# Most of the latents' projection put behind the context's queries in the order of work, and three modulations of the second layer put into the first half of the gates

## The chip, the cores and the metric

The kernel runs on one core of one Trainium2 chip. It is written by hand for the core's engines: TensorE (PE, matrix products; its weight loads are listed as PEld), VectorE (DVE), ScalarE (ACT), GpSimd (POOL) and SyncE (SP), which issues most of the DMAs. Each engine takes its instructions strictly in the order in which they were laid down and waits at each until its operands are there. The metric is the device time of one execution in microseconds; lower is better. Three runs of the kernel before took 2460.11, 2469.60 and 4105.28 us; their median is 2469.6 us.

## The reference

Two layers of a backbone are applied to two groups of tokens that share all weights: 128 context tokens (one block of 128) and 256 latent tokens (two blocks). Everything is float32, and the model width is D = 1024. One layer computes, for either group:

```
mod = silu(cond) @ w_mod[l] + b_mod[l]           # six rows of D: shift1 scale1 gate1 shift2 scale2 gate2
h   = LN(x) * (1 + scale1) + shift1
p   = h @ w_in[l]                                # 1024 -> 1696 columns, for three mixers
A   = GQA attention, 8 query and 2 kv heads      # latents also attend to cached context keys
B   = multi-head latent attention, 4 heads
C   = chunked spatial-gating MLP
x   = LN(ALPHA*x + gate1 * (concat(A,B,C) @ w_o[l]))
h2  = LN(x) * (1 + scale2) + shift2
x   = LN(ALPHA*x + gate2 * PEER(h2))
```

PEER is a layer of 128 x 128 = 16384 single-neuron experts. For each token and each of 8 heads it forms a query `h2 @ w_q`, scores its two halves against 128 keys each, takes the best 16 of either, the best 16 of their 256 sums, and from these a softmax gate g. Then `out = sum over the 128 chosen experts of g * gelu(u[expert] . h2) * v[expert]`. The tables `u` and `v` are 16384 x 1024 for each layer. The outputs are the two groups' x after both layers and the context's new keys and values.

## The kernel before

**Two ways of computing PEER.** For the 128 context tokens only the chosen experts' rows are read: once the expert numbers `ids` are known (line 676), POOL issues 128 indirect DMAs for `u` (line 686), each of which brings one row of 4 KB for each of 128 tokens (512 KB) into one of four buffers `gt`, and DVE multiplies each with the context's `h2c` and sums it up (line 692, called a u_step below). Later 128 more such gathers bring rows of `v` (line 703). For the 256 latents the whole tables are streamed. The phase that goes through the first half of `u` is called phase A (`a_step`: SP loads, ACT and DVE split each block into a high and a low part, PE multiplies it with `h2T`, three passes, tile `psA`, line 854). Then 32 steps `w_step(0, n)` turn the gates of the first half of the experts into a dense matrix (tile `psW`, line 893) and multiply it in, in the first gate half; the product with `v` (`o_step`, tile `acc`, line 930) begins after them, and second halves of both follow.

**Order in a layer.** In a layer, the context's chain and the latents' chain run beside each other. The context's steps are marked as urgent (`hp()`): projection (`p`), attention (`a`), output projection and norm (`o`, line 522, tile `psoc`), then in `ctx_picks` the transposed and modulated h2 (line 201, tile `m2pst`), its queries (line 561, tile `psqp`, 16 chunks of `w_q`), the choice of experts (lines 546 to 643) and `ids`. The latents' projection `pl_` consists of 14 chunks of 128 columns of `w_in` (line 262, tile `psil`, one load `wil` a chunk; the last chunk has 32 columns). How many of them are written ahead of which of the context's steps is said by a string, `ORD` for the first layer and `ORD1` for the second: each `l` is one chunk, each digit one modulation of the first layer. What is left of the projection comes behind `ctx_picks` by `run(pl_)`. Then the latents' attention (lines 421 to 452, scores in `pssl`), output projection (line 522, tile `psol`; DVE takes each result at line 524) and second norm (line 147 on DVE and line 149 on ACT, tile `m2xh`) follow, then their queries with 16 more loads `wq`, routing, and phase A.

**Modulations.** A modulation is one of the six rows `mod`: 8 loads `wm` of 512 KB and 64 short matmuls (line 166, tile `psm`). Those of the second layer are taken from a list; `MB` of them are written ahead of the latents' attention of the first layer, the others later, one in each eighth step of a gate half.

**What sets the order.** A scheduler sorts the written steps by their urgency and a simulated time line into one fixed list for each engine. So an instruction stands behind all that were laid before it on its engine, also where they have nothing to do with each other: an attention step of the latents on DVE behind a u_step waits for that u_step's gather. All loads of weights go through SP's queue in one order, into a ring of six buffers of 512 KB (line 157); the context's `w_in` and `w_o` of the second layer have two buffers of their own. On POOL the first 50 gathers of the first layer and the first 60 of the second are free to go as soon as a buffer is free; each later one is tied to a mark in the latents' work (line 1028, `N0`). The store of the latents' x for the end of the layer (line 949, `xd`) stands in POOL's list among the gathers.

Of the kernel before, what the change touches and what calls it, by code (L numbers as in the profile page):

```python
# [45 lines left out]
def tile_fn(ctx: ExitStack, tc, A, outs):  # L46
# [17 lines left out]
    def psum(es, spec):  # L64

        for tag, n in spec.items():
            banks[tag] = pool(es, f"ps_{tag}", n, space=PSUM)

    def pS(tag, name):
        return banks[tag].tile([128, 512], F32, name=name, tag=tag)  # L70
# [575 lines left out]
    def out_c(cc):  # L646
        with ExitStack() as e1:
            cc.out_proj(e1)
# [100 lines left out]
    mods = []  # L749
    for l in range(DEPTH):  # L750
        last = l + 1 == DEPTH

        with ExitStack() as es3:
            psum(es3, BK[min(l, 1)])
            with ExitStack() as esc:
# [11 lines left out]
                def first():  # L767
                    run(project(l, cc))
                    if l == 0:
# [7 lines left out]
                       "a": lambda: cc.attention_in(esc), "o": lambda: out_c(cc)}  # L777
                for k in (ORD if l == 0 else ORD1):
                    if k == "l":
# [7 lines left out]
                if not last:  # L787
                    mods = [(l + 1, v) for v in (1, 0, 2, 4, 3, 5)]
                    for _ in range(MB):
                        modulation(*mods.pop(0), "m")  # L790
# [5 lines left out]
        with ExitStack() as es_:  # L796
# [158 lines left out]
            X = pool(es6, f"x{l}", 2)  # L955
            ar.append(pool(es6, f"at{l}").tile([128, NS - HALF, 256], F32, name="AR2"))
            psum(esP, {"acc": 4})
            accp = [[pS("acc", "acc") for _ in range(2)] for _ in range(2)]
            for n in range(NW):
                w_step(0, n)  # L960
                if (n + 1) * PRE // NW > n * PRE // NW:
                    a_step(NA + n * PRE // NW)
            for ii in range(PRE, NA):
                o_step(ii - PRE)
                a_step(NA + ii)
# [36 lines left out]
            for k, r in RATES[l].items():  # L1002
                ms = marks[k]
                n = int(len(ms) * r + 0.5)
# [22 lines left out]
CQ = 0  # L1027
RATES = [{'L':0.25,'A':1,'W':0.01,'B':2,'X':1,'O':2.125}, {'L':0.125,'A':0.875,'W':0.01,'B':2.375,'X':0.5,'O':2.625}]
N0 = [50,60]
MB = 5  # L1030
ORD1 = 'paollllllllllllll'
ORD = 'p2ll4ll3llaollllllll'
HP = 100000
KA = 0.125
KO = 0
# [92 lines left out]
```

## Time and profile before

| | before |
|---|---|
| median of three runs | 2469.6 us |
| profiled execution, own time | 2466.42 us |
| span of the profiled execution | 2464.7 us |
| granted clock of TensorE, mean | 0.961 of full speed |
| PE busy | 2267.0 us (92%) |
| DVE busy | 1959.7 us (80%) |
| ACT busy | 1166.0 us (47%) |
| POOL busy | 695.4 us (28%) |
| read from memory | 689.14 MB, 281 GB/s over the span |

All times in the rows below count from the first instruction of the profiled execution. What the execution's time adds to the span is 1.7 us. Busy time is the time in which an engine's own instructions ran; a share near one in a stretch says that the engine sets the pace there, a low share that it waits. In a timeline, the number in brackets is the engine's idle time just ahead of the row, with the instruction or DMA that ended it. Rows of equal instructions in sequence are drawn together, with their count at the end.

### The profile page before, as it was taken

To read this page: it belongs to the slowest core of one execution; us is meant where nothing else is said; L and a number is where in the kernel's file an instruction comes from. 1 tells how busy PE (TensorE), PEld (TensorE's weight loads), DVE (VectorE), ACT (ScalarE), POOL (GpSimd) and SP (SyncE) were. 2 spreads that over 40 slices of the span, in tenths; PEclk is the share of its full clock that TensorE was granted. 3 is DMA by queue.
4 is the path that set the end of the run, shared out by engine and by line. 5 is a ranking of instruction groups with operands and counts; after the bars stand their busy time and mean duration, and the time that the engine had idled before them with its cause. 6 is when DMAs were issued, how large, how long until landed. Compare 5 with 4: busy or idle time off the path is not lost. (4 is left out here: it accounts for less than half of the span.)

```text
span 2464.7 us, 42531 instructions
## 1 busy us (share of the span) xinstructions
PE 2267.0 (92%) x15980; PEld 1932.8 (78%) x15980; DVE 1959.7 (80%) x3995; ACT 1166.0 (47%) x2143; POOL 695.4 (28%) x523
## 2 busy tenths in 40 slices
PE   6999889899999999999989978689999999998997
PEld 5696568789997886677778856579999889965886
DVE  2157579997897889998853577899869888899987
ACT  3324422444785445544445342325448744465444
POOL 0000233443004554355100005432210053344640
PEclk8999989999999998999998989899999999998999
DMA  9857899889547999899763528888984499987994
GB/s 328 314 192 258 341 328 342 322 309 342 204 155 269 367 356 379 284 332 390 266 214 95 174 87 280 316 307 286 317 291 153 155 348 366 339 314 271 388 372 145
DMA packets 196318, 696.10 MB, mean 282 GB/s; under 512 B 22992, under 2 KB 27408, under 8 KB 196112
## 3 DMA queue, kind: packets, MB, share of 16 engines
q1 hardware_dynamic: 110016, 398.52, 45.3%
q0 software_dynamic: 74736, 272.14, 30.7%
q10 hardware_dynamic: 11360, 22.73, 2.7%
q8 instruction: 125, 2.05, 0.3%
q14 instruction: 81, 0.66, 0.1%
HBM read 689.14 MB, written 4.16 MB: 281 GB/s over the span
## 5 line engine op out<-in xcount | busy, mean ns | idle before, releaser
L686 POOL DMA_INDIRECT gt<-in_peer_u_dram,ids x256 | 303.0, 1183 | 1274.2 <-DVE ids L676 544.1
L854 PE MATMUL psA<-h2hi,ulo 128*128 128x256 f32 x1920 | 555.0, 289 | 32.3 <-DVE ulo L847 32.3
L854 PE MATMUL psA<-h2hi,uhi 128*128 128x256 f32 x1920 | 548.3, 286 | 5.6 <-ACT uhi L846 3.7
L854 PE MATMUL psA<-h2lo,uhi 128*128 128x256 f32 x1920 | 546.2, 284 | 0.0
L930 PE MATMUL acc<-vhi,pp 128*128 128x512 f32 x1856 | 521.1, 397 | 17.4 <-ACT pp L909 11.1
L686 POOL DMA_INDIRECT gt<-in_peer_v_dram,ids x256 | 388.1, 1516 | 432.3 <-DVE acc L703 383.1
L930 PEld LDWEIGHTS acc<-vhi,pp 128*128 128x128 f32 x1856 | 349.8, 191 | 93.8 <-ACT pp L909 11.6
L846 ACT ACTIVATE uhi<-u 128x1024 fp32r<-128x1024 f32 x240 | 254.5, 1060 | 345.9 <-PE psA L854 215.8
L854 PEld LDWEIGHTS psA<-h2hi,ulo 128*128 128x128 f32 x1920 | 370.7, 193 | 41.4 <-DVE ulo L847 40.9
L918 ACT ACTIVATE vhi<-v 128x1024 fp32r<-128x1024 f32 x232 | 246.1, 1061 | 319.6 <-PE acc L930 200.5
L854 PEld LDWEIGHTS psA<-h2hi,uhi 128*128 128x128 f32 x1920 | 370.8, 193 | 9.2 <-ACT uhi L846 4.7
L847 DVE TENSOR_TENSOR ulo<-u,uhi 128x1024 fp32r<-128x1024 f32 x240 | 292.7, 1219 | 106.4 <-ACT uhi L846 105.4
L854 PEld LDWEIGHTS psA<-h2lo,uhi 128*128 128x128 f32 x1920 | 370.6, 193 | 1.4
L703 DVE SCALAR_TENSOR_TENSOR acc<-gt,wcol,acc 128x1024 f32<-128x1024 f32 x254 | 324.5, 1278 | 7.5 <-DMA gt<-in_peer_v_dram,ids 6.7
L692 DVE SCALAR_TENSOR_TENSOR gt<-gt,h2c 128x1024 f32<-128x1024 f32 x256 | 309.7, 1214 | 23.3 <-DMA gt<-in_peer_u_dram,ids 21.9
L919 DVE TENSOR_TENSOR vlo<-v,vhi 128x1024 fp32r<-128x1024 f32 x232 | 282.7, 1220 | 57.2 <-ACT vhi L918 55.2
L930 PE MATMUL acc<-vlo,pp 128*128 128x512 f32 x928 | 295.9, 400 | 8.6 <-DVE vlo L919 7.5
L930 PEld LDWEIGHTS acc<-vlo,pp 128*128 128x128 f32 x928 | 174.3, 191 | 51.7 <-DVE vlo L919 15.0
L875 ACT ACTIVATE e<-iota,nid 128x128 f16<-128x128 f16 x512 | 158.8, 428 | 62.2 <-PE psW L893 62.0
L561 PE MATMUL psqp<-h2T,wq 128*128 128x256 f32 x512 | 119.6, 388 | 0.3 <-DVE h2T L207 0.3
L262 PE MATMUL psil<-wil,hT 128*128 128x128 f32 (+1 forms) x896 | 111.5, 276 | 0.8 <-ACT proj L263 0.5
L900 DVE SCALAR_TENSOR_TENSOR AR<-psW,AR 128x256 f32<-128x256 f32 (+2 forms) x256 | 96.0, 415 | 20.2 <-PE psW L893 20.0
(435 smaller groups left out, 2897.1 us busy)
## 6 DMA issues: line engine op xcount, KB each, us to landing
u<-in_peer_uT_dram SPq DMA_DIRECT2D x256, 512.0 KB
v<-in_peer_v_dram SPq DMA_DIRECT2D x256, 512.0 KB
wm<-in_w_mod_dram SPq DMA_DIRECT2D x96, 512.0 KB
wq<-in_peer_wq_dram SPq DMA_DIRECT2D x64, 512.0 KB
wic<-in_w_in_dram SPq DMA_DIRECT2D x26, 512.0 KB
wil<-in_w_in_dram SPq DMA_DIRECT2D x26, 512.0 KB
woc<-in_w_o_dram SPq DMA_DIRECT2D x16, 512.0 KB
wol<-in_w_o_dram SPq DMA_DIRECT2D x16, 512.0 KB
```

The costliest lines, as they stand in the source:

```text
L262: T.matmul(ps[:, :n], lhsT=ch.hT[b][:, c, :], rhs=wv[:, c, :], start=(c == 0), stop=(c == 7))
L561: T.matmul(ps[:, :n * 128], lhsT=wv[:, c, :], rhs=hT[:, c, :], start=(c == 0), stop=(c == 7))
L686: nc.gpsimd.indirect_dma_start(out=t, out_offset=None, in_=tab, in_offset=bass.IndirectOffsetOnAxis(ap=pk.ids[:, j:j + 1], axis=0))
L692: V.scalar_tensor_tensor(t, t, 1.0, pk.h2c, op0=OP.mult, op1=OP.mult, accum_out=acol[:, j:j + 1])
L703: V.scalar_tensor_tensor(pk.acc, t, wcol[:, j:j + 1], pk.acc, op0=OP.mult, op1=OP.add)
L846: S.activation(hi, ua, AF.Copy)
L847: marks["A" if ii < NA else "U" if ii < NA + PRE else "B"].append(V.tensor_sub(lo, ua, hi.bitcast(F32)))
L854: T.matmul(ps[:, a * 256:(a + 1) * 256], lhsT=lw[:, c * 128:(c + 1) * 128], rhs=rw[:, c, :], start=(k == 0), stop=(k == 8 * len(passes) - 1))
L875: S.activation(e2[:, t // TI, :, t % TI], iota1, AF.Abs, bias=nb_[:, t0 % 128 + t:t0 % 128 + t + 1])
L918: S.activation(hi, v, AF.Copy)
L919: marks["O" if ii >= NA else "Q" if ii >= NA - PRE else "P"].append(V.tensor_sub(lo, v, hi.bitcast(F32)))
L930: T.matmul(accp[tb][h], lhsT=pl[:, tb * 128:(tb + 1) * 128], rhs=vr[:, h * 512:(h + 1) * 512], start=(i == 0 and k == 0), stop=(i == 127 a ...
```

## The change

Four numbers and three lines of code change; lines after 960 move down by two.

```diff
@@ -955,11 +955,13 @@
             psum(esP, {"acc": 4})
-            accp = [[pS("acc", "acc") for _ in range(2)] for _ in range(2)]
             for n in range(NW):
                 w_step(0, n)
                 if (n + 1) * PRE // NW > n * PRE // NW:
                     a_step(NA + n * PRE // NW)
+                if n % 8 == 3 and len(mods) > 1:
+                    modulation(*mods.pop(0), "acc")
+            accp = [[pS("acc", "acc") for _ in range(2)] for _ in range(2)]
             for ii in range(PRE, NA):
@@ -1027,9 +1029,9 @@
-MB = 5
-ORD1 = 'paollllllllllllll'
-ORD = 'p2ll4ll3llaollllllll'
+MB = 2
+ORD1 = 'paollll'
+ORD = 'p2l4l3laolll'
```

In the first layer 6 of the 14 chunks of the latents' projection now stand ahead of the context's second norm and queries, not 14; in the second layer 4, not 14. The others come behind `ctx_picks` and ahead of the latents' attention. Of the second layer's modulations two, not five, stand ahead of the latents' attention in the first layer; three more come at n = 3, 11 and 19 of the first gate half, and the sixth in the second gate half as before. A modulation in the first gate half writes its sums to the four banks of `acc`, which is why `accp` is now taken behind that loop. No instruction is added or left out.

The scheduler turns this into new lists. Three places are shown, each row an instruction as `line operation output<-inputs shape`, with a count where equal ones follow one another.

On PE in the first layer, where the context's queries end, the list before ran the last pieces of the projection (`psil`) between the queries (`psqp`, scores `pssk`) and went on to the latents' scores (`pssl`):

```order
L561 MATMUL psqp<-h2Tc,wq_1755 128x128 x8
L262 MATMUL psil<-wil_1361,hT_536 128x32
L262 MATMUL psil<-wil_1361,hT_537 128x32 x3
L566 MATMUL pssk<-kT_1431,qp 128x128
L561 MATMUL psqp<-h2Tc,wq_1778 128x128 x8
L262 MATMUL psil<-wil_1361,hT_537 128x32 x4
L566 MATMUL pssk<-kT_1431,qp 128x128
L262 MATMUL psil<-wil_1361,hT_537 128x32
L421 MATMUL pssl<-kTl,qTl 128x384
```

Now, after the last query chunk (`wq_1602`), seven and a quarter chunks of projection and one modulation (`psm`) follow:

```order
L561 MATMUL psqp<-h2Tc,wq_1602 128x128 x8
L262 MATMUL psil<-wil_1734,hT_537 128x128 x4
L566 MATMUL pssk<-kT_1255,qp 128x128
L262 MATMUL psil<-wil_1734,hT_537 128x128 x4
L262 MATMUL psil<-wil_1756,hT_536 128x128 x8
L566 MATMUL pssk<-kT_1255,qp 128x128
L262 MATMUL psil<-wil_1756,hT_537 128x128 x8
L262 MATMUL psil<-wil_1778,hT_536 128x128 x4
```

The queries now run almost without projection between them, and `pssl` comes behind the last chunk (`wil_1888`) and the eight loads of modulation 1. In the second layer the same holds with nine and a quarter chunks and no modulation.

On DVE in the first layer, around the latents' first output projection (`psol`, line 524), the list before had these rows; the u_steps are those of line 692:

```order
L692 SCALAR_TENSOR_TENSOR gt,acol<-gt,h2c 128x1024
L423 TENSOR_REDUCE mx<-pssl 128x1
L171 TENSOR_TENSOR modrow<-psm,bm 128x256
L443 COPY pT<-psT 128x3x128
L427 RECIPROCAL sums<-sums 128x2
L692 SCALAR_TENSOR_TENSOR gt,acol<-gt,h2c 128x1024
L181 COPY cols_102<-psc 128x8 x2
L692 SCALAR_TENSOR_TENSOR gt,acol<-gt,h2c 128x1024
L524 TENSOR_TENSOR y_2840<-psol,g_2838 128x128
```

Now there are:

```order
L443 COPY pT<-psT 128x3x128
L692 SCALAR_TENSOR_TENSOR gt,acol<-gt,h2c 128x1024
L423 TENSOR_REDUCE mx<-pssl 128x1
L692 SCALAR_TENSOR_TENSOR gt,acol<-gt,h2c 128x1024
L427 RECIPROCAL sums<-sums 128x2
L692 SCALAR_TENSOR_TENSOR gt,acol<-gt,h2c 128x1024 x4
L524 TENSOR_TENSOR y_2664<-psol,g_2662 128x128
L524 TENSOR_TENSOR y_2665<-psol,g_2662 128x128
```

Counted from the start of the list, 8 u_steps stood ahead of the first row of line 524 and now 42; ahead of the latents' `m2xh` 19 and now 50; at the end of phase A 114 in either. In the second layer these are 15 and now 48, and 33 and now 60. POOL's list has 54 gathers ahead of the first `xd` store in the first layer, not 21, and 64 in the second, not 33.

On PE in the first gate half the second part of the first of the three modulations (`wm_2...`) now stands between two products of the gates (`psW`), and the other two later in the same way:

```order
L893 LDWEIGHTS e_5757
L893 MATMUL psW<-e_5759,e_5757 128x64
L166 MATMUL psm<-wm_22_5865,silu 32x256 x3
L166 MATMUL psm<-wm_23_5871,silu 32x256 x4
L166 MATMUL psm<-wm_24_5877,silu 32x256 x4
L166 MATMUL psm<-wm_25_5883,silu 32x256 x4
L166 MATMUL psm<-wm_26_5889,silu 32x256 x4
L166 MATMUL psm<-wm_27_5895,silu 32x256 x4
L893 LDWEIGHTS e_5907
L893 MATMUL psW<-e_5909,e_5907 128x64
```

Before, no row of line 166 stood there. On SP the loads go along: the first layer's queue had the 40 loads `wm` of five modulations between the context's `wq` and the `wol` of the latents' output projection, and has 16 now; the 24 others stand between the loads of `u` of the first gate half.

## Rows read from the trace of the kernel before

**Rows 1.** Page, parts 1 and 4: busy engines; chain of waits by engine.

```profile
PE 2267.0 (92%) x15980; PEld 1932.8 (78%) x15980; DVE 1959.7 (80%) x3995; ACT 1166.0 (47%) x2143; POOL 695.4 (28%) x523
...
PE 23%; DVE 8%; issue 4%; DMA 2%; POOL 2%; ACT 1%; DVEq 0%; POOLq 0%; ACTq 0%
```

**Rows 2.** Windows, layer 0 (columns: stretch, then each engine's busy us).

```profile
213.00:255.00 42.00, 39.72 (x312) 17.81 (x312) 34.48 (x161) 27.19 (x61) 0.00 (x0) 0.96 0.79 295
...
255.00:302.00 47.00, 41.55 (x278) 23.11 (x278) 24.58 (x61) 23.63 (x61) 13.02 (x12) 1.00 0.93 352
...
350.00:637.00 287.00, 266.77 (x1836) 252.86 (x1835) 256.38 (x716) 110.05 (x151) 112.54 (x92) 0.97 0.90 326
...
637.00:745.00 108.00, 105.56 (x1263) 104.66 (x1261) 98.81 (x177) 93.14 (x191) 0.00 (x0) 1.00 0.48 152
```

**Rows 3.** Timeline of PE, layer 0 (start us, us, instruction).

```profile
151.75 7.76 PE L262 MATMUL psil<-wil,hT 128*128 128x128 f32 x68
...
159.34 1.04 PE L201 MATMUL m2pst<-ident,m2xh 128*128 128x128 f32 x8
...
165.69 1.95 PE L561 MATMUL psqp<-h2Tc,wq 128*128 128x128 f32 x16
...
209.61 0.47 PE L566 MATMUL pssk<-kT,qp 128*128 128x128 f32 x2
...
210.15 0.91 PE L421 MATMUL pssl<-kTl,qTl 64*128 64x384 f32 x2
...
214.80 4.29 PE L166 MATMUL psm<-wm,silu 128*32 128x256 f32 x48
```

**Rows 4.** Timeline of SyncE's queue, layers 0 and 1: loads of weights.

```profile
200.28 76.51 SPq L157 DMA_DIRECT2D wm<-in_w_mod_dram  x40
...
1318.42 32.70 SPq L157 DMA_DIRECT2D wil<-in_w_in_dram  x8
```

**Rows 5.** Timeline of DVE, layer 0.

```profile
255.37 0.28 DVE L676 TENSOR_TENSOR ids<-i,i 128x128 int32<-128x128 f32 x1
...
303.79 0.29 DVE L524 TENSOR_TENSOR y<-psol,g 128x128 f32<-128x128 f32 x1 [5.01 <-PE psol L522]
...
336.14 0.81 DVE L147 TENSOR_SCALAR m2xh<-xl,m_mv,m_rs 128x1024 f32<-128x1024 f32 x1
```

**Rows 6.** Timeline of PE, layer 0: first matmul of the gates.

```profile
637.51 0.66 PE L893 MATMUL psW<-e,e 128*128 128x64 f16 x16
```

**Rows 7.** Timeline of PE and DVE, layer 1.

```profile
1387.66 1.07 PE L201 MATMUL m2pst<-ident,m2xh 128*128 128x128 f32 x8
...
1389.28 0.88 PE L421 MATMUL pssl<-kTl,qTl 64*128 64x384 f32 x2 [0.40 <-DVE gs L469]
...
1482.89 0.29 DVE L676 TENSOR_TENSOR ids<-i,i 128x128 int32<-128x128 f32 x1
...
1515.45 0.48 DVE L524 TENSOR_TENSOR y<-psol,g 128x128 f32<-128x128 f32 x2
...
1559.95 0.81 DVE L147 TENSOR_SCALAR m2xh<-xl,m_mv,m_rs 128x1024 f32<-128x1024 f32 x1
...
1846.42 0.66 PE L893 MATMUL psW<-e,e 128*128 128x64 f16 x16
```

**Rows 8.** Timeline of POOL, layer 1: gathers.

```profile
1483.45 0.93 POOL L686 DMA_INDIRECT gt<-in_peer_u_dram,ids  x1 [291.21 <-DVE ids L676]
...
1493.53 1.82 POOL L686 DMA_INDIRECT gt<-in_peer_u_dram,ids  x1 [1.14 <-DVE gt L692]
...
1547.93 1.02 POOL L686 DMA_INDIRECT gt<-in_peer_u_dram,ids  x1 [0.61 <-DVE la_rs L118]
```

**Rows 9.** Windows, layer 1.

```profile
1485.00:1545.00 60.00, 49.59 (x339) 40.82 (x338) 47.81 (x109) 13.47 (x33) 33.37 (x30) 0.94 0.88 302
...
1568.00:1848.00 280.00, 267.43 (x1868) 252.29 (x1867) 243.01 (x690) 109.74 (x151) 81.68 (x78) 0.98 0.86 303
```

**Rows 10.** Tile psm: what its engine waited for, us and times.

```profile
  DMA wm<-in_w_mod_dram: 46.9, 38
```

## The prediction

> **What bounds the kernel now.** I read the page first, then windows by stage, then the timelines of PE and DVE around the stages that the change touches, and last POOL's gathers. The page has PE busy 92% of the span, and the chain that ended last runs over PE for 23% and DVE for 8% [rows 1]. The windows show that this mean hides different stages [rows 2]. Between 213 and 255 us PE is busy 39.72 of 42 us: projection, queries and modulations set the pace. From 255 to 302 it is busy 41.55 of 47, DVE only 24.58, and the DMAs are at 0.93 with 352 GB/s. In phase A and the queries before it (350 to 637) PE is busy 266.77 of 287 and DVE 256.38, so either one delays the other. In the first gate half (637 to 745) PE is busy 105.56 of 108 and the DMAs only 0.48. So the change takes loads out of a stretch where they are dense and puts matmuls into one where PE has 2.4 us to spare.
>
> The points by which I measure are, in layer 0: the context's second norm reaches PE (`m2pst`) at 159.34, latents' scores begin at 210.15 [rows 3], `ids` at 255.37, first result of the latents' output projection at 303.79, latents' `m2xh` at 336.14 [rows 5], gates at 637.51 [rows 6]. In layer 1 the same points are 1387.66, 1389.28, 1482.89, 1515.45, 1559.95 and 1846.42 [rows 7].
>
> **Durations.** 68 matmuls of the projection start over 7.59 us (151.75 to 159.34) [rows 3], 0.112 us each; a chunk has 32, so 3.57 us. A query chunk of the context is 1.95 us and its score product up to 0.47 [rows 3]; I take 2.2. Modulation: 48 records `psm` in 4.29 us, 64 would be 5.7; where its loads are there, it is a little less, and I take 5 us. Gathers: 33 went out from 1483.45 to 1547.93 [rows 8], 64.48 / 32 = 2.015 us apart, with the DMAs at 0.88 and 302 GB/s in that stretch [rows 9]. That is the pace of gathers when nothing but gathers and the latents' attention runs, and I use it for the new lists, which ask for such a run in both layers.
>
> **Layer 0, up to the latents' second norm.** Three chunks fewer are loaded and multiplied ahead of the context's output projection and its norm; 3 x 3.57 is 10.7 us of PE, of which part filled gaps in the context's chain. I put `m2pst` 8 us earlier, at 151. From there to the first query before were 6.3 us (159.34 to 165.69), which I leave as they are; the 16 chunks of queries take 35, then 7.25 chunks of projection 26, one modulation 5, small transposes 2 to 5. Latents' scores begin at about 228 instead of 210. `ids` on DVE stands now behind the first score reductions, so it can't come before about 235, 20 us earlier than before. From there on, in-order DVE ties the latents' attention to the gathers: `m2xh` stands behind 50 u_steps. 235 + 49 x 2.015 + 12 for the last gather to land and the norm is 346; by the output projection, 42 u_steps ahead of it end at about 322 and the way from there to `m2xh` was 32 us before (303.79 to 336.14), now perhaps 30, that is 352. I take 350: **+14**. Bounds: if the gathers keep ahead of the attention, only PE decides; of the 126 us from 210.15 to 336.14 the three modulations (15 us) and some waiting for loads go, so that 228 + 100 = 328 to 330, **-6**. Above, 2.35 us a gather (the 76 us from `ids` to `m2xh` in layer 1 over its 33 u_steps [rows 7]) gives 367, **+31**.
>
> **Layer 0, from there to the gates.** This took 301.4 us (336.14 to 637.51). Now 64 u_steps are left of those in phase A, not 95; 31 times 524 KB of gathers, 16 MB, and 31 x 1.2 us of DVE leave a stretch in which DVE is busy 256.38 of 287 and the DMAs 0.90. Then PE sets the pace: 266.77 us busy, and 9 us from `m2xh` to the first query (as in layer 1, 1559.95 to about 1568 [rows 7, 9]), 276 in all, so at most 25 us can go. I take **-23**; the other end is -8, if the waits are for ACT's and SP's work and not for DVE's.
>
> **First gate half.** Three modulations on a PE that is 98% busy: 3 x 5 - 2.4 = 12.6 us at least. Their 24 loads (12.6 MB) stand in the ring of six between loads of `u`, with DMAs at 0.48; but each modulation eats 8 buffers in 5 us where loading 4.2 MB takes 12 us at 352 GB/s. Six of eight may lie ready, the last two and the first `u` behind them are late. In the whole run PE waited 46.9 us for `wm` in 12 modulations [rows 10], 3.9 each. So the ends are +12 and 3 x (5.7 + 3.9) = +29, and I take **+16**, near the lower, since PE's list puts products of the gates between the pieces.
>
> **Layer 1.** Before, eight loads `wil`, issued over 32.70 us from 1318.42 [rows 4], stood in SP's queue ahead of the context's last `w_o` and queries. They now stand behind. I put the context's `m2pst` 20 us earlier, at 1368 (the ends are 5 and 30). Then 6 + 35 for the queries and 9.25 x 3.57 = 33: latents' scores at 1442, not 1389, `ids` at 1448, not 1483. `m2xh` behind 60 u_steps: 1448 + 59 x 2.015 + 12 = 1579, **+19** (ends 0 and +35, by the same two cases). From `m2xh` to the gates were 286.5 us, PE busy 267.43 of the 280 in the window [rows 9]; with 9 at its head the least is 276, and 27 u_steps fewer should give it: **-10** (ends -4 and -10).
>
> **Sum:** +14 - 23 + 16 + 19 - 10 = +16 on the profiled execution's 2466.42, so 2482 us. That execution is 3 us under the median of the runs, 2469.6; in terms of the median the change is +13 or 0.5%. A difference within 2% (49 us) is about what a measurement of this kernel can tell from none; by it the forecast is "no change".
>
> **A rule against the row.** In the gather row at 1493.53 POOL needs 1.82 us where the one at 1483.45 needs 0.93 [rows 8]; it began just after a u_step of DVE had. The Trainium skill ("SBUF — State Buffer", section "Who interferes with whom") says why dense u_steps may hurt: a DVE instruction with two inputs in SBUF and a GpSimd instruction that reads SBUF exclude each other for the whole instruction. The trace agrees with that. It is the mechanism of the second rival.
>
> **Rivals.**
> *The gathers run ahead.* If DVE never waits for one, `m2xh` comes as early as PE allows, and the freed phase A is kept: -6 - 25 + 12 + 0 - 10 = -29, about 2437 us. For it: only 12 gathers ran from 255 to 302 (POOL busy 13.02) [rows 2], held by DVE's list and not by bandwidth; and 12.6 MB of `wm` leave. Against it: in layer 1, with no modulations, gathers came only every 2.015 us. The Trainium skill ("DMA: Bandwidth & Descriptors", section "Anatomy of one DMA — SWDGE (gpsimd) path") gives a fixed 2.0 us and bytes at 436 GB/s: as an estimate from that page the moving part of a 512 KB gather is 1.2 us, so 42 of them in some 50 us instead of 83. The run at 2.015 us speaks against it, though other loads ran beside.
>
> *Dense u_steps lock POOL.* If each gather meets a u_step, as at 1493.53, its issue takes 1.82 + 0.30 and the loop through four buffers stretches to 2.35 us a gather or more. Then `m2xh` is +31 in layer 0 and +35 in layer 1, and the gate half loses its upper price: 31 - 23 + 29 + 35 - 10 = +62, about 2528 us, slower by 2.4%. It decides from about 2.3 us a gather on. For it: 8 of the 33 gathers in that run took 1.3 us or longer. Against it: the mean over these is already 2.015.
>
> *It cancels.* The same matmuls, loads and u_steps are done in another order, and what phase A gains, the gate half costs: 2466, the profiled time. For it: PE is busy 92% [rows 1] and idles in layer 0 only some 40 us between 159 and 637.
>
> **Chances and range.** Forecast (2470 to 2500) 0.48, gathers ahead 0.22, cancelled 0.16, lock 0.14. The range must take in most of the first and part of the lock: 2436 to 2518. Faster by over 2% (under 2420) needs more than the first rival with all its bounds: 0.07. Slower by over 2% (above 2519): most of the lock's cases, 0.12. The rest, 0.81, lies within 2%.
>
> **What would show it.** In the new profile `ids` near 235 and 1448; gathers 1.9 to 2.1 us apart after them; DVE idle ahead of line 692 for the DMA `gt` rather than on `psol`; `m2xh` near 350 and 1579; gates of layer 0 some 278 us and of layer 1 276 us after it; line 166 between the gates, and the first `acc` product about 124 us after the first `psW`, where it was 108. I am wrong if the attention isn't held by gathers (`m2xh` near 330), if phase A keeps its 301 us although the u_steps left it, or if the three modulations cost 30 us or nothing where they now stand.

## The result and the profile after

The changed kernel took 2523.35 us (median of four runs, 2519.49 to 2528.2) against 2470.1 us, a ratio of 1.0239 with a 95% interval of 1.0218 to 1.026. One of the four runs of the kernel before was a slow one (4105.28 us); the ratio is of the fast runs alone, so that it is not the quotient of these two medians. The changed kernel is slower by 53 us by the medians, where 2482 was forecast with a range up to 2518. The profiled execution took 2526.06 us; its span is 2524.2, 59.5 more than before.

From the page of the changed kernel: busy engines, the chain of waits by engine, and the group of the gathers of `u`.

```profile
PE 2298.9 (91%) x15980; PEld 1952.1 (77%) x15980; DVE 1962.6 (78%) x3995; ACT 1176.1 (47%) x2147; POOL 699.8 (28%) x523
...
PE 47%; issue 13%; DVE 9%; DMA 5%; POOL 4%; ACT 3%; DVEq 0%; ACTq 0%; POOLq 0%
...
L686 POOL DMA_INDIRECT gt<-in_peer_u_dram,ids x256 | 304.4, 1189 | 1313.5 <-DVE gt L692 564.0
```

PE ran the same 15980 instructions, but was busy 32 us longer than before [rows 1]. The chain that ended last runs over PE for 47% of the span, 23% before; it could be followed further back, and by itself does not say where the loss is. The mean time of a gather on POOL is 1189 ns, 1183 before.

Windows of the changed kernel in layer 0: the latents' attention in two pieces, queries and phase A, the first gate half. The columns, here and in rows 2, are the stretch and its length, the busy time of PE, PEld, DVE, ACT and POOL (with the number of instructions), the mean granted clock of TensorE as a share of 2.4 GHz, the busy share of the DMA engines, and GB/s.

```profile
214.00:260.00 46.00, 34.18 (x174) 15.10 (x167) 27.78 (x74) 27.41 (x62) 14.74 (x13) 0.88 0.73 271
...
260.00:300.00 40.00, 26.05 (x82) 14.36 (x83) 26.25 (x56) 13.69 (x36) 17.21 (x17) 0.63 0.76 250
...
361.00:647.00 286.00, 269.98 (x1892) 252.92 (x1884) 233.05 (x671) 123.20 (x182) 72.18 (x65) 0.97 0.82 287
...
647.00:780.00 133.00, 127.37 (x1452) 116.47 (x1452) 100.85 (x188) 94.04 (x192) 0.00 (x0) 0.95 0.64 218
```

From 214 to 300 PE is now busy 34.18 of 46 and 26.05 of 40 us, at a granted clock of 0.88 and 0.63; before, it was busy 41.55 of 47 at 1.00 in the corresponding stretch [rows 2]. The first gate half (647 to 780) keeps PE nearly as busy as before and is 25 us longer; its clock is 0.95 and was 1.00.

Timelines of DVE and PE of the changed kernel at the points of rows 5 and 6, and the first product with `v`:

```profile
225.40 0.29 DVE L676 TENSOR_TENSOR ids<-i,i 128x128 int32<-128x128 f32 x1
...
329.61 0.54 DVE L524 TENSOR_TENSOR y<-psol,g 128x128 f32<-128x128 f32 x2
...
360.68 0.81 DVE L147 TENSOR_SCALAR m2xh<-xl,m_mv,m_rs 128x1024 f32<-128x1024 f32 x1
...
646.96 0.66 PE L893 MATMUL psW<-e,e 128*128 128x64 f16 x16
...
780.27 1.09 PE L930 MATMUL acc<-vhi,pp 128*128 128x512 f32 x4
```

And the points of rows 7, in layer 1:

```profile
1400.47 1.97 PE L201 MATMUL m2pst<-ident,m2xh 128*128 128x128 f32 x8 [8.10 <-DVE m2xh L147]
...
1478.23 1.65 PE L421 MATMUL pssl<-kTl,qTl 64*128 64x384 f32 x2
...
1488.82 0.28 DVE L676 TENSOR_TENSOR ids<-i,i 128x128 int32<-128x128 f32 x1
...
1597.92 0.48 DVE L524 TENSOR_TENSOR y<-psol,g 128x128 f32<-128x128 f32 x2
...
1634.23 0.81 DVE L147 TENSOR_SCALAR m2xh<-xl,m_mv,m_rs 128x1024 f32<-128x1024 f32 x1
...
1906.35 0.66 PE L893 MATMUL psW<-e,e 128*128 128x64 f16 x16
```

The differences from before, taken from these rows; the first column of numbers is what the prediction's terms said:

| step | forecast | measured |
|---|---|---|
| layer 0, latents' `m2xh` | +14 | +24.5 (336.1 to 360.7) |
| `m2xh` to the gates | -23 | -15.1 (301.4 to 286.3) |
| first gate half, to the first product with `v` | +16 | +24.9 (108.4 to 133.3) |
| rest of layer 0, to its last product with `v` | 0 | -4.9 |
| layer 1, from there to the latents' `m2xh` | +19 | +44.9 (285.4 to 330.3) |
| `m2xh` to the gates | -10 | -14.4 (286.5 to 272.1) |
| sum, up to the gates of layer 1 | +16 | +59.9 |

The signs are right, and every loss is larger than forecast; the largest miss is layer 1's +45 in place of +19.

### The profile page after: what moved, and what is told of

It reads as the page before. It is cut to its first block, busy times and chain, and to the rows that moved or that the text cites. A ratio compares the mean times of both kernels' runs of the same rounds, so it can differ in the third digit from the quotient of the medians.

```text
span 2524.2 us, 42580 instructions
## 1 busy us (share of the span) xinstructions
PE 2298.9 (91%) x15980; PEld 1952.1 (77%) x15980; DVE 1962.6 (78%) x3995; ACT 1176.1 (47%) x2147; POOL 699.8 (28%) x523
## 4 chain that ended last, share of the span: by engine, by line
PE 47%; issue 13%; DVE 9%; DMA 5%; POOL 4%; ACT 3%; DVEq 0%; ACTq 0%; POOLq 0%
PE acc L930 21%; PE psA L854 17%; POOL gt L686 4%; PE psqp L561 3%; DMA gt<-in_peer_u_dram,ids 2%; DMA gt<-in_peer_v_dram,ids 2%; DVE acc L703 1%; PE psW L893 1%; DVE ulo L847 1%; DVE gt L692 1%; PE psic L262 1%; DVE AR L900 1%; PE psil L262 1%; DVE vlo L919 1%; DVE e L886 1%
## 5 line engine op out<-in xcount | busy, mean ns | idle before, releaser
L686 POOL DMA_INDIRECT gt<-in_peer_u_dram,ids x256 | 304.4, 1189 | 1313.5 <-DVE gt L692 564.0
```

The lines of the kernel that those rows point to most:

```text
L686: nc.gpsimd.indirect_dma_start(out=t, out_offset=None, in_=tab, in_offset=bass.IndirectOffsetOnAxis(ap=pk.ids[:, j:j + 1], axis=0))
```

## The experiments

All times are medians, and each ratio is against runs of the kernel before on the same chip.

**The three parts apart.** Each is the kernel before with one part of the change.

```diff
# second_only
-ORD1 = 'paollllllllllllll'
+ORD1 = 'paollll'
# first_only
-ORD = 'p2ll4ll3llaollllllll'
+ORD = 'p2l4l3laolll'
# gates_only: MB = 2 and the lines of the change in the first gate half
```

> The kernel before with the second layer's order alone (ORD1 with 4 chunks ahead). Two theories of why the change costs 53 us. List: with the latents' attention put later, DVE's list has 48 multiply-and-sum steps of the context's gathers ahead of the latents' first output projection (15 before), and the attention waits behind them for gathers. Late start: the attention only begins later, because ten chunks of the projection stand between the context's queries and it, and the gathers beside it are free. By either, the second layer's part of the loss shows here, as the trace of the changed kernel has it: +25 to +35 us on 2470, so 2495 to 2505; latents' m2xh in layer 1 near 1604 (before 1560), 48 such steps ahead of line 524. If the loss of layer 1 needs the first layer's change as well, within 10 us of before.

Measured: 2493.8 us, ratio 1.0112 (1.0076 to 1.0148). As both theories had it, the loss shows here: the gates of layer 1 came 30 us later than before.

> The kernel before with the first layer's order alone (ORD with 6 chunks ahead, five modulations still ahead of the latents' attention). DVE's list has 28 of the context's multiply-and-sum steps ahead of the latents' m2xh in layer 0 (19 before, 50 with the whole change). List theory: a small change, 0 to +12 us, 2470 to 2482, as few steps are added. Late-start theory: the projection behind the queries costs nearly its 20 us in the first layer here too, of which phase A gives nothing back: 2485 to 2495.

Measured: 2465.29, ratio 1.0005 (0.9983 to 1.0027). `m2xh` of layer 0 came at 349.89 (+13.8), and the gates at 639.70 (+2.2). It fits the list theory; the late-start theory had counted on 20 us, but the latents' scores began only 8 us later than before: the context's second norm came 19 us earlier, and the way from it to the scores, with the chunks on it, grew by 27 us (50.8 to 77.6). The same move puts the scores off by more in layer 1. There they didn't wait for the context's queries before: they began 1.6 us after the context's `m2pst` [rows 7], and 77.8 us after it in the changed kernel.

> The kernel before with MB = 2 and the three modulations in the first gate half, orders of both layers as before. DVE's list has 43 of the context's multiply-and-sum steps ahead of the latents' m2xh in layer 0 (19 before). The first gate half grows by 20 to 25 us (15 us of matmuls and some waiting). By the list theory m2xh does not come earlier although 15 us of modulations are gone ahead of it, and phase A gets 10 to 15 us shorter: +5 to +15 in all, 2475 to 2485. By the late-start theory m2xh comes 10 to 15 us earlier and phase A is shorter as well: -5 to +3, 2465 to 2473.

Measured: 2492.65, ratio 1.0111 (1.0076 to 1.0145). Both expectations were too low. The half became 21 us longer, and `m2xh` came 21 us *later* although 15 us of matmuls had left; phase A gave 15 of these back (286.1 us for 301.4):

```profile
210.51 0.91 PE L421 MATMUL pssl<-kTl,qTl 64*128 64x384 f32 x2
...
321.59 0.29 DVE L524 TENSOR_TENSOR y<-psol,g 128x128 f32<-128x128 f32 x1 [0.94 <-PE psol L522]
...
356.86 0.97 DVE L147 TENSOR_SCALAR m2xh<-xl,m_mv,m_rs 128x1024 f32<-128x1024 f32 x1
...
642.94 0.66 PE L893 MATMUL psW<-e,e 128*128 128x64 f16 x16
...
772.58 1.09 PE L930 MATMUL acc<-vhi,pp 128*128 128x512 f32 x4
```

The three parts make 1.0112 x 1.0005 x 1.0111 = 1.0229; the whole change is 1.0239. So the first layer's order costs nothing by itself, and the second layer's order and the modulations cost nearly 30 us each.

**Gathers held back in the changed kernel.** A gather that is tied to the latents' first query takes its u_step behind `m2xh`.

```diff
+                if NH[l] <= j < N0[l]:
+                    with tc.issue_after(marks["L"][0].ins):
+                        f()
-                if j < N0[l] or j - N0[l] >= len(hold):
+                elif j < N0[l] or j - N0[l] >= len(hold):
+NH = [20,33]
```

> The changed kernel with 30 gathers of layer 0 (the 21st to the 50th) and 27 of layer 1 (the 34th to the 60th) tied to the latents' first query, so that they stand behind the latents' m2xh; 20 and 33 multiply-and-sum steps are left ahead of it, as many as before the change. Late start and all else as in the changed kernel. List theory: latents' m2xh in layer 1 comes 30 us earlier than in the changed kernel (about 1600 of its time), in layer 0 some 15 earlier; phase A of each layer takes about 10 us more; 2490 to 2505, 20 to 35 us under the changed kernel. Late-start theory: m2xh stays where it is and phase A grows by 10 in each layer: 2523 to 2545.

Measured: 2543.99, ratio 1.0329 (1.0293 to 1.0364), slower than the changed kernel. The list theory was right on the place: `m2xh` of layer 1 came 25 us earlier, counted from the end of layer 0 (305.0 us after it, 330.3 in the changed kernel), in layer 0 18 us earlier. It was wrong on the whole: phase A grew by 31 us in layer 0 (286.3 to 317.4) and by 28 in layer 1 (272.1 to 299.7) and took it all back. The late-start theory had it the other way round, wrong on the place and right on the whole. Moving the steps in DVE's list wins nothing.

**Layer 1 without any step ahead.** `NH = [50,0]` with the lines above, in second_only and in the kernel before.

> second_only with all of layer 1's 60 free gathers tied to the latents' first query: no multiply-and-sum step and no gather stands ahead of the latents' m2xh, so that the stretch from the latents' first scores to the first result of their output projection shows the attention alone (117 us in second_only with 48 steps ahead). List theory: 75 to 88 us without them. Late-start theory: 95 to 110 us, most of it the attention's own chain of PE, DVE and ACT, that ran beside the context's queries and routing before. Clock theory: 95 to 110 us too, with a clock of 0.75 or less. In all of them phase A takes over 60 steps and gets 35 to 50 us longer: 2500 to 2525 in all.

Measured: 2512.1, ratio 1.02 (1.0175 to 1.0225). The rows are first scores, first result of the output projection, `m2xh`, first gates:

```profile
1448.70 0.91 PE L421 MATMUL pssl<-kTl,qTl 64*128 64x384 f32 x2
...
1532.29 0.29 DVE L524 TENSOR_TENSOR y<-psol,g 128x128 f32<-128x128 f32 x1 [8.73 <-PE psol L522]
...
1559.08 0.81 DVE L147 TENSOR_SCALAR m2xh<-xl,m_mv,m_rs 128x1024 f32<-128x1024 f32 x1
...
1890.85 0.66 PE L893 MATMUL psW<-e,e 128*128 128x64 f16 x16
```

The attention alone took 83.6 us, 117 in second_only with 48 steps in between, as the list theory said. But the 60 steps made phase A 332 us long; in second_only it was 273:

```profile
1450.11 1.65 PE L421 MATMUL pssl<-kTl,qTl 64*128 64x384 f32 x2
...
1567.27 0.28 DVE L524 TENSOR_TENSOR y<-psol,g 128x128 f32<-128x128 f32 x1
...
1603.14 0.81 DVE L147 TENSOR_SCALAR m2xh<-xl,m_mv,m_rs 128x1024 f32<-128x1024 f32 x1
...
1876.52 0.66 PE L893 MATMUL psW<-e,e 128*128 128x64 f16 x16
```

So a step costs 44.1 / 60 = 0.73 us ahead of `m2xh` and 58.4 / 60 = 0.97 behind it. It has to be paid in either place. The 0.73 needn't be DVE's list alone: from the scores to line 524 the granted clock was 0.70 with the steps and 0.88 without, and PE was busy 89.26 us and 68.08 with the same work. No run separates the two.

> The kernel before with all of layer 1's 60 free gathers tied to the latents' first query, as in second_heldall: no multiply-and-sum step ahead of the latents' m2xh in layer 1 in either of the two, so that they differ by the order of the projection alone. Late-start theory: the order before still wins by 25 to 30 us without any such step in the way: m2xh near 1535, gates of layer 1 near 1865, 2480 to 2490 in all against 2512. List theory (the steps ahead of m2xh are what the new order loses by): the two are then alike, m2xh near 1555, gates near 1888, 2505 to 2515.

Measured: 2488.68, ratio 1.0108 (1.0086 to 1.0129). The same four rows:

```profile
1384.18 0.88 PE L421 MATMUL pssl<-kTl,qTl 64*128 64x384 f32 x2 [0.28 <-DVE gs L469]
...
1501.45 0.29 DVE L524 TENSOR_TENSOR y<-psol,g 128x128 f32<-128x128 f32 x1 [8.72 <-PE psol L522]
...
1528.25 0.81 DVE L147 TENSOR_SCALAR m2xh<-xl,m_mv,m_rs 128x1024 f32<-128x1024 f32 x1
...
1863.44 0.66 PE L893 MATMUL psW<-e,e 128*128 128x64 f16 x16
```

Here no step stands ahead of `m2xh` in either kernel, and the order before still reaches it 31 us earlier and the gates 27 us earlier; the medians are 23 us apart, against 30 with the steps. 5 of the 27 us lie ahead of layer 1 in these two executions. So the late start carries about three quarters of layer 1's loss, and what the steps do to the attention the rest. The late-start theory holds, and I drop the list as the main cause.

What the late start does is seen in two pairs of windows, first of the kernel before (layer 1, context's queries with the latents' scores; routing):

```profile
1387.66:1452.00 64.34, 60.72 (x396) 47.31 (x395) 37.37 (x162) 34.16 (x98) 0.00 (x0) 0.97 0.45 140
...
1452.00:1483.00 31.00, 19.31 (x61) 9.70 (x59) 26.98 (x132) 14.37 (x31) 0.00 (x0) 0.67 0.10 35
```

then of second_only (queries; projection; attention behind `ids`; phase A):

```profile
1371.50:1412.00 40.50, 37.26 (x303) 36.67 (x304) 23.54 (x108) 9.10 (x34) 0.00 (x0) 0.89 0.61 190
...
1412.00:1450.00 38.00, 37.03 (x327) 36.84 (x326) 34.92 (x175) 13.71 (x40) 0.00 (x0) 0.99 0.43 135
...
1460.50:1567.00 106.50, 82.07 (x269) 43.04 (x268) 77.13 (x157) 44.30 (x113) 61.65 (x51) 0.72 0.78 254
...
1603.00:1876.50 273.50, 264.84 (x1853) 251.59 (x1853) 218.27 (x646) 117.89 (x170) 56.44 (x54) 0.98 0.78 263
```

Before, the dense queries and the sparse attention shared the 64 us from 1388, PE busy 60.72. Now queries and projection run first, dense, and the attention follows nearly alone: 82 us of PE in 106.5 at a clock of 0.72. The three engines wait for each other there: PE 10.0 us for ACT's `qm`, ACT 11.0 for DVE's `sums` and 7.8 for PE's `psT`, DVE 7.7 for PE's `pssl`; and DVE waits 17.4 us for gathers.

**Half of the chunks.**

```diff
-ORD1 = 'paollllllllllllll'
+ORD1 = 'paolllllllll'
```

> The kernel before with nine chunks of layer 1's projection ahead and five behind (14 and 0 before, 4 and 10 in second_only). DVE's list has 40 and 58 multiply-and-sum steps ahead of line 524's first row and of m2xh, nearly as in second_only (48 and 60; 15 and 33 before). Late-start theory: half of the chunks behind, some half of the loss, 2474 to 2482. List theory: nearly the same list, nearly the same loss, 2486 to 2495.

Measured: 2493.64, ratio 1.0116 (1.0096 to 1.0135), the full loss with five chunks behind, as the list theory had it. By the trace it fits the late start as well, and my guess that the loss goes by chunks was what failed: the attention can't begin before the last chunk, its scores began at 1442.87 (1450.11 in second_only, 1389.28 before), and the context's second norm, which is what the move is to bring forward, came at 1386.07, hardly earlier than before. This run doesn't tell the two apart.

**The clock.** PE's granted clock was low where the attention ran. 192 short matmuls, `silu` with a weight in SBUF, were written behind the latents' attention of layer 1. (A modulation has 32 such matmuls in the kernel, four for each of its 8 loads; the trace shows each as two records, which is where the 64 of the section on the kernel before come from.)

```diff
+                fill(NF[l], Wl)      # NF = [0, 192]
                 lat.out_proj()
```

> second_only with 192 short matmuls more in the latents' attention of layer 1 (the shape of a modulation's, of data already in SBUF, into a bank that nobody reads; 27 us at full clock). In second_only TensorE's granted clock is 0.72 from 1460 to 1567 and PE is busy 22 us longer over layer 1 than before with the same instructions. Clock theory: with PE fed, the clock in that stretch is 0.9 or more, the way from ids to the first result of the output projection shrinks from 107 to 85 to 95 us, and the whole is 2478 to 2486, against 2494. List theory (the multiply-and-sum steps on DVE pace the attention; 60 stand ahead of line 524's first row here): no gain, 2494 to 2510, and the clock rises without use. Late-start theory: no gain either, and some of the 27 us on top, 2500 to 2515.

Measured: 2509.46, ratio 1.018 (1.0152 to 1.0209). Windows of second_only and, below, of second_fill with its first scores, its first result of the output projection and `m2xh`:

```profile
1460.00:1500.00 40.00, 35.19 (x87) 15.51 (x86) 28.33 (x61) 18.06 (x48) 22.02 (x19) 0.63 0.70 226
...
1500.00:1540.00 40.00, 26.77 (x85) 14.46 (x86) 28.12 (x58) 14.33 (x37) 21.30 (x19) 0.70 0.85 285
```

```profile
1457.66 1.64 PE L429 MATMUL pssl<-kTl,qTl 64*128 64x384 f32 x2
...
1455.00:1500.00 45.00, 44.73 (x356) 19.02 (x356) 33.26 (x71) 20.81 (x54) 26.35 (x24) 0.96 0.82 271
...
1500.00:1540.00 40.00, 23.45 (x92) 11.70 (x90) 29.50 (x61) 11.74 (x32) 24.51 (x21) 0.74 0.83 279
...
1582.51 0.29 DVE L532 TENSOR_TENSOR y<-psol,g 128x128 f32<-128x128 f32 x1 [0.32 <-PE psol L530]
...
1609.31 0.81 DVE L147 TENSOR_SCALAR m2xh<-xl,m_mv,m_rs 128x1024 f32<-128x1024 f32 x1
```

In the first piece the clock rose from 0.63 to 0.96. The result came at 1582.51, not 1567.27, but this row has 60 steps ahead of it here and 48 there, and the scores began 8 us later. Ahead of `m2xh` stand 60 steps in both, and from the scores to `m2xh` were 151.7 us here and 153.0 in second_only: nothing was won. That doesn't show that the low clock is free. The fill ended at 1503, it kept PE busy for 44.73 of the 45 us of the first piece, and what the clock gave back there may have gone into the fill.

> The kernel before with the same 192 matmuls in the latents' attention of layer 1, where the clock was 0.67 from 1452 to 1483 and PE idle for about 12 us. Clock theory: that stretch gets up to 8 us shorter and the fill finds room in the gaps: 2455 to 2466, the same as before or a little faster. List and late-start theories: no gain, 2465 to 2485, as the fill takes PE's time where attention wants it.

Measured: 2463.51, ratio 1.0002 (0.9987 to 1.0018). The fill found room, and nothing was won; 39 steps stood ahead of `m2xh` here, 33 before.

**Layer 0: why `m2xh` is late without the modulations.**

> gates_only with the 21st to 50th gather of layer 0 tied to the latents' first query: 20 multiply-and-sum steps ahead of the latents' m2xh (43 in gates_only, 19 before). List theory: m2xh of layer 0 comes back from 357 to 325 to 337, with 15 us of modulations less ahead of it than before; phase A takes 10 to 28 us more than in gates_only; 2490 to 2502 in all, the gate half 21 us longer than before as in gates_only. If it is not the steps that hold it: m2xh 350 or later.

Measured: 2522.68, ratio 1.0225 (1.0183 to 1.0268). A miss: `m2xh` stayed at 358.51. `ids` came 10 us later (265.14), and the 20 steps left stood in the middle of the attention, all of them ahead of line 524's first row. So I went down to the number that stood ahead of that row before the change.

```diff
# gates_held8: gates_only with the lines above and
+NH = [8,60]
# gates_held8_fill: the same, and fill(96) behind the attention of layer 0
```

> gates_only with the 9th to 60th free gather of layer 0 tied to the latents' first query: 8 multiply-and-sum steps ahead of line 524's first row in layer 0, as in the kernel before (28 in gates_only, 20 in gates_held). From the latents' first scores to that row were 94 us before with 8 steps, 111 in gates_only, 117 in gates_held. List theory: 80 to 95 us with 8. Clock theory (without the modulations' matmuls PE's clock falls to 0.7 and each link of the chain takes longer): 100 us or more, clock under 0.85 in that stretch. Phase A gets longer by the steps moved there; 2520 to 2535 in all.

Measured: 2508.6, ratio 1.0181 (1.014 to 1.0223), two runs.

```profile
210.67 0.91 PE L421 MATMUL pssl<-kTl,qTl 64*128 64x384 f32 x2
...
304.82 0.29 DVE L524 TENSOR_TENSOR y<-psol,g 128x128 f32<-128x128 f32 x1 [8.72 <-PE psol L522]
...
333.87 0.81 DVE L147 TENSOR_SCALAR m2xh<-xl,m_mv,m_rs 128x1024 f32<-128x1024 f32 x1
...
667.24 0.66 PE L893 MATMUL psW<-e,e 128*128 128x64 f16 x16
```

With 8 steps, scores to first result are 94.15 us, 111 with 28. Before, it was 93.6 with 8 steps *and* three modulations more [rows 3, 5]. The modulations' 15 us of matmuls had cost nothing there: they lay in the gaps of the attention. The steps held back are paid behind: phase A took 333.4 us, 301.4 before.

> gates_held8 with 96 short matmuls (as many as three modulations have, of data in SBUF, without loads) behind the latents' attention in the order of work, so that they fall into its gaps. Clock theory: the way from first scores to line 524's first row comes down to 94 us or less, the clock to 0.9 or more, m2xh 10 us or more earlier than in gates_held8. List theory: the same as gates_held8 within 4 us or a few us later.

Measured: 2514.33, ratio 1.0205 (1.0158 to 1.0251), two runs; scores to first result took 9 us more than in gates_held8 (314.68 - 211.60 = 103.1 us). The granted clock over this way was 0.92, 0.89 in gates_held8 and 0.98 before, so the fill hardly raised it; that 0.89 without the fill took the same 94 us as 0.98 before speaks against the clock theory in layer 0. The fill also shows a limit: 96 short matmuls cost 9 us where the 96 of the modulations had cost nothing. They lay between 235 and 275 us, those of the modulations from 215 on; whether this is the reason wasn't tried.

**The gate half.**

```diff
# gate_fill: the kernel before, five modulations left where they were
                     a_step(NA + n * PRE // NW)
+                if l == 0 and n in (3, 11, 19):
+                    fill(32)
# gates_thin: gates_only with
-            for k in range(4):
+            for k in range(1 if thin and 0 < c < 7 else 4):
```

> The kernel before with 3 x 32 short matmuls more at n = 3, 11 and 19 of the first gate half of layer 0: the number and shape of the three modulations' matmuls, but of data that is in SBUF already, without loads; the five modulations stay ahead of the latents' attention. If the gate half's price is PE's matmuls: 13 to 16 us longer, 2476 to 2481 in all. If it is loads and their ring: up to 5 us longer, 2464 to 2469. In gates_only the half became 21 us longer; what is over 15 there is the loads' part.

Measured: 2472.07, ratio 1.0041 (1.002 to 1.0061). First gate and first product with `v`:

```profile
633.75 0.66 PE L902 MATMUL psW<-e,e 128*128 128x64 f16 x16
...
754.41 1.09 PE L939 MATMUL acc<-vhi,pp 128*128 128x512 f32 x4
```

The half took 120.7 us, 12 more than before: 96 matmuls at 0.13. But 7.5 of these came back on the way from the first product with `v` to the last of layer 0.

> gates_only with all 24 loads of the three modulations in the first gate half but only 42 of their 96 matmuls (the results of these modulations are incomplete). In gates_only the half took 129.6 us (108.4 before), with the matmuls alone 120.7. If the rest is the loads' part (ring of six, more bytes): 120 to 125 us here, and at the end of layer 0 still some 12 to 16 us over before: 2477 to 2484 in all, against 2492. If the matmuls are the cost: 112 to 116 us, 2468 to 2475.

Measured: 2474.25, ratio 1.005 (1.003 to 1.0071).

```profile
638.44 0.66 PE L893 MATMUL psW<-e,e 128*128 128x64 f16 x16
...
759.46 1.09 PE L930 MATMUL acc<-vhi,pp 128*128 128x512 f32 x4
```

This kernel leaves out 54 of the 96 matmuls. All loads and the other 42 made the half 121.0 us, 12.6 more than before, and 9.6 came back later. In the half the loads have a price of their own, as the expectation had it: 42 matmuls at gate_fill's 0.127 are 5.3 of the 12.6 us, which leaves 7.3 for what comes with the loads, and 12.2 + 7.3 = 19.5 is near gates_only's 21.2. In the whole time the two don't add so: by the medians either alone costs 7 to 10 us, and gates_only 29. In these two the way from the first product with `v` to the last of layer 0 was 7.5 and 9.6 us shorter than before, in gates_only 0.9. In the other executions with the three modulations in the half it was 3.5 to 9.8 us shorter, so gates_only's 0.9 may be that execution's; it wasn't settled.

The clock has a part in the half too. Two windows of the changed kernel, then the whole half of gates_held8_fill, which has the same three modulations there:

```profile
660.00:670.00 10.00, 7.22 (x80) 6.39 (x74) 8.45 (x16) 7.07 (x14) 0.00 (x0) 0.75 0.92 342
...
700.00:710.00 10.00, 8.23 (x81) 7.32 (x82) 6.36 (x12) 6.91 (x13) 0.00 (x0) 0.66 0.82 288
...
680.90:807.90 127.00, 122.57 (x1455) 111.68 (x1454) 101.13 (x188) 94.27 (x192) 0.00 (x0) 1.00 0.65 228
```

In the changed kernel PE waited 2.7 us in all behind the first modulation, most of it for the split blocks of `u`, and 2.9 us around the second, 1.5 of it for a load `wm`; both times the clock then fell to its lower level. In gates_held8_fill it stayed at the upper level and the half took 127.0 us. The other halves with these modulations line up by their clock: gates_only 129.6 us at 0.99, gates_held8 130.8 and gates_held 131.1 at 0.97, held and the changed kernel 133.3 at 0.95. So where PE is full, the lower clock costs its time: about 6 of the changed kernel's 25 us. Why it fell in one and not in the other is open: PE was as idle in gates_held8_fill from 690 to 700 (7.21 of 10 us busy).

**A try at better than both.**

```diff
-MB = 5
+MB = 6
```

> The kernel before with MB = 6: also the sixth modulation of the second layer ahead of the latents' attention of layer 0, none in a gate half. If modulations fill gaps there that cost nothing, and cost their 5 us or more in a gate half (three cost 21 us in gates_only): 5 to 8 us faster, 2456 to 2460. If they cost the same in either place: 2462 to 2466. If the 8 loads more delay the attention's own loads: up to 2472.

Measured: 2462.98, ratio 0.9997 (0.9983 to 1.0011), no difference. Layer 0 ended 7.9 us earlier: one modulation less in the second gate half. Layer 1's new list lost half of that: its `m2xh` came 11.5 us earlier than before, but phase A took 296.1 us, 9.7 more. No kernel that ran beats the one before.

## Why the prediction was wrong

**The latents' second norm is the step that failed**, in layer 1 above all. The prediction had: `m2xh` behind 60 u_steps at the pace of gathers, 1448 + 59 x 2.015 + 12. It let the gathers alone decide and the attention run beside them for nothing. Both go through DVE's one list, and each made the other longer. In the forecast's own terms, the 26 us that layer 1 misses by are these: `ids` came 184.7 us after the end of layer 0, not 173 (+11); the 60 gathers went out 2.17 us apart, not 2.015 (+9); and what lies ahead of the first and behind the last of them was 18 us, not 12 (+6). In layer 0 `ids` came 10 us earlier than forecast, and from there to `m2xh` were 135.3 us, not 115: 50 gathers 2.33 us apart. From `ids` to `m2xh` DVE waited 24.1 us for gathers in layer 0 and 27.5 in layer 1, as the forecast had it, but POOL waited 26.4 us in layer 1 for u_steps to free a buffer, and u_steps stood behind the attention's instructions.

What fits is a sum, with the measured pieces: scores at 1478, 84 us of attention alone, 27 to `m2xh` (1532.29 to 1559.08), 60 steps at 0.73 = 44, together 1633; the trace has 1634.23. The 0.73 is from second_only, which has the same order in layer 1, so this shows only that the two agree. A check apart from it is held, with 33 steps: 84 + 27 + 24 = 135 from scores to `m2xh`, measured 131. The forecast of the start itself was good: the scores 53 us later than before, measured 59.6 against the end of layer 0. It gave this start no price, as it took `m2xh` from `ids` and the gathers; before_heldall shows that the start is the larger part of the loss.

**The lower bound was wrong too.** Layer 0's "-6" took the modulations' 15 us off the attention. gates_held8 shows that they were in its gaps: without them, and with as many steps, it took 94.15 us for 93.6. So their leaving freed nothing ahead of the gates.

**The gate half.** The mechanism was right: matmuls on a PE that has no room cost their full time, 12 us alone, and their loads came on top, some 7. The size was 25 (21 with the order of before), not 16; about 6 of it is the lower clock, which the prediction didn't reckon with.

**Phase A** got shorter, as forecast, by 15 and 14 us; in layer 0 I had 23. The forecast let PE wait for only 9 us. In layer 0 it was busy 270.18 of the 286.2 us, so it still waited for 16; before, it was busy 272.55 of 301.4. In layer 1, 263.56 of 272.1, the waits came down to 9, and the stretch is shorter than the 276 that I took for the least.

**The rivals.** *The gathers run ahead* is out: DVE waited for gathers in 50 places in the two stretches. *Dense u_steps lock POOL* had a time near the measured one (2528), and the pace came near the 2.3 us a gather that it asked for, 2.33 in layer 0 and 2.17 in layer 1; but its mechanism did not decide. 14 of 54 and 22 of 64 gathers in the two layers of the changed kernel took 1.3 us or more to issue, 8 of 33 before [rows 8]; over all gathers of `u` the mean rose by 6 ns; and in layer 1 POOL was busy for 81.25 of the 145.5 us from `ids` to `m2xh`, so its issuing did not set the pace. The rule on the shared port ("SBUF — State Buffer", section "Who interferes with whom", of the Trainium skill) may well be at work in those rows. By the mean, what the change added is some 1.5 us in 256 gathers. *It cancels* holds for the first layer's order alone (1.0005).

**The range** ended at 2518. Its upper bounds, +31, +29 and +35, were each about right or too low (measured +24.5, +24.9 and +44.9), but I treated them as unlikely to meet. Two don't follow from their own terms: 235 + 49 x 2.35 + 12 is 362, +26 and not +31, and 1448 + 59 x 2.35 + 12 is 1599, +39 and not +35; the sum stays nearly the same. They met, and I think because they have one cause: PE's dense work was taken from beside a stage that is a chain of short waits, and put ahead of it, or into a stage that has no gaps.

## What to carry to other kernels

A stage that is a chain over several engines wants dense work of others beside it: moving that work ahead of the chain starts the chain late, and moving it into a stage where PE is full costs its whole time. To price a stage behind a move, add its own length to its new start and then add for what else stands in the same in-order list; don't take the larger of the two. A step that took 1.21 us on DVE added 0.73 here, as part of it fell into waits. A kernel in which a delayable step is held back shows whether the step is a cause or only a place where the loss shows: here the loss moved from the norm to phase A and stayed.

## What the hardware showed

PE's granted clock was at one of two levels, 1.2 and 2.4 GHz, and a mean such as 0.63 is a mix of both over a stretch. It was 1.00 from 255 to 302 us before, with modulations between the attention's matmuls and PE busy 41.55 of 47 us [rows 2], and 0.63 from 260 to 300 in the changed kernel, with PE busy 26.05 of 40. Summed over the trace, PE worked 181 us at the lower level in the changed kernel and 125 before; at half the pace that is 28 of PE's 32 us of longer busy time. It misleads: busy shares of 70 to 80% in such a stretch are partly slow matmuls. Raising the clock with idle matmuls (0.63 to 0.96) brought no time back in the attention, where the fill itself took PE. In the first gate half, where PE is full, two falls of the clock cost about 6 us (133.3 for 127.0).
